# DeltaNet values transposed on VectorE through DRAM, and an instruction order laid with stored shifts of its deadlines

## The chip, the cores and the metric

The kernel runs on one core of one Trainium2 chip. The metric is the device time of one execution in microseconds (us), taken as the median over the runs shown. Differences are told against the kernel before the change, which ran on the same chip.

## The reference, cut to what matters

One layer of a decoder: 1024 tokens, width 2048, one input projection, three head groups, one output projection, and a final RMSNorm. All data are float32.

```
h = rmsnorm(x) ;  P = h @ W_in                       # columns: gMLP, DeltaNet, cross-attention
qkv = silu(causal_conv(concat(d_q, d_k, d_v)))       # depthwise, 4 taps
q, k = l2norm(q) * 128**-0.5, l2norm(k)              # 8 heads x 128
# gated delta rule over chunks, state S (128 x 128) per head:
v_new = val_c - kcd_c @ S ;  o_c = qg_c @ S + attn_c @ v_new
S = S * exp(g_last) + kd_c.T @ v_new
out_b = rmsnorm(o) * silu(d_z)
x = x + concat(out_a, out_b, out_c) @ W_out ;  y = rmsnorm(x)
```

The scan reads the values v with the tokens on the partitions, scaled per token. The convolution makes them with the channels on the partitions, so that they have to be transposed once, per head and half sequence.

## The kernel before, in words

**Matrix products.** The two large projections are seven-product (Strassen) schemes over halves of the tokens and of the columns. Each float32 factor is split into a rounded high part and a low part, and a product is three matmuls of 128x512 (high by high, high by low, low by high). The names in the trace: `raw` and `kept` are weight blocks as loaded from DRAM, `rhi` and `rlo` their split, `ll`, `lm`, `lh` the split left factors, `acc` (four) and `dn` (four) the eight PSUM banks, `obs`, `yu`, `yz` the finished sums of a projection stage. TensorE runs one product after the other; ScalarE rounds the high parts, VectorE takes the differences and adds up the seven products, and the SyncE queue (SP) issues nearly all the transfers.

**Stages.** Memory and token rows are prepared first (about 0 to 100 us). Then come the projections of the first four and the last four DeltaNet heads, a stage for the gate columns and the gMLP values (it ends near 917 us), one for the gMLP input and gate, one for the cross-attention, and the output projection. The DeltaNet work of a pair of heads and a half sequence (`hf`) is laid between the products of those stages: `front` (convolution of q and k, norms, the 128x128 matrices), `inverse` (a chain of small VectorE steps on `inv` and `sq` that solves 32x32 blocks), `levels`, `values` (the convolution of v and its transpose), `scan_step` and `heads_out`. There are eight such pairs, so sixteen calls of the convolution for v.

**Values before.** `conv` loads a head's projected columns into a buffer of the ring `xr`, forms the four taps into a buffer of the ring `tn` (one ScalarE and three VectorE instructions) and applies SiLU on ScalarE. `to_tokens` transposes the four 128x128 blocks on TensorE into a PSUM bank, and `by_token` scales them from PSUM into `vs` on ScalarE, from where the scan reads them.

**A second way to transpose, already there.** `turn` transposes the 32x32 blocks of a tile in one VectorE instruction and stores the result in DRAM with one transfer; `turned_in` reads it back with four transfers that put the blocks in their places. `heads_out` takes the scan's output through it (DRAM tensors `od`), from token rows to channel rows; `four` is the view of a tile as 4 by 4 blocks.

**What sets the order.** All instructions are recorded first (`Plan.add`) with a price. `Plan.lay` then lays them with a list scheduler: on each engine the ready instruction with the smallest key goes first. The key is the deadline that `Plan.late` works out backwards from the last order. `Plan.issue` repeats this eight times, keeps the shortest order by the planner's own costs, and emits the instructions in it, engine by engine. Each engine then works strictly in that order and waits for semaphores. Every recorded instruction carries the line of `issue` (L398) in the profile, so groups are told apart by tile names.

Of the kernel before, what the change touches and what calls it, by code (L numbers as in the profile page):

```python
# [11 lines left out]
AF = mybir.ActivationFunctionType  # L12
# [5 lines left out]
P = 128  # L18
# [4 lines left out]
HT = 512  # L23
# [3 lines left out]
NG, NH, NX = 4, 8, 4  # L27
# [26 lines left out]
class Engine:  # L54
    def __init__(self, plan, eng, ns):
        self.plan, self.eng, self.ns = plan, eng, ns
# [6 lines left out]
class Plan:  # L63
# [3 lines left out]
    DMA_RATE = 350.0  # L67
    DMA_FIXED = 3800.0
    SWITCH = 250.0
    FIRST, SPREAD, PASSES, STRETCH, AHEAD = 0, 1.75, 8, 1.25, 1000.0  # L70
    TABLE, HOLD = 1300.0, 6000.0

    def __init__(self, nc):
        self.ops = []
# [247 lines left out]
    def late(self, preds):  # L322
# [56 lines left out]
                    heapq.heappush(soon[lead.eng], (ready[lead.idx], lead.idx))  # L379
        return goal  # L380

    def issue(self):
        preds = [[] for _ in self.ops]
        for o in self.ops:
            for s in o.succ:
                preds[s.idx].append(o)
        best = None
        key, hold = [o.cls for o in self.ops], 0.3
        for n in range(self.FIRST + self.PASSES + 1):
            end = self.lay([o.cls * 1.0e9 + o.idx if o.cls < 0 else k for o, k in zip(self.ops, key)], hold)  # L390
            if best is None or end < best[0]:
                best = end, [o.at for o in self.ops]
            key, hold = self.latest() if n < self.FIRST else self.late(preds), self.HOLD
        for o, o.at in zip(self.ops, best[1]):
            pass
        self.ops.sort(key=lambda o: (o.at, o.idx))
        for o in self.ops:
            o.fn(*o.args, **o.kw)  # L398
# [3 lines left out]
def kernel(  # L402
# [21 lines left out]
    x, mem, w_in, out = x[0], mem[0], w_in[0], out[0]  # L424
# [56 lines left out]
    def tok(ap):  # L481

        return ap.rearrange("p (t c) -> p t c", c=P)
# [22 lines left out]
    jk = C([P, HT], "jk", mybir.dt.bfloat16)  # L506
# [4 lines left out]
    turn = {"acc": 0, "tp": 0, "dn": 0}  # L511
# [224 lines left out]
    for mt in range(2):  # L736
        t = [ring["ai"](F32R) for _ in range(2)]
# [9 lines left out]
    for h in range(NX):  # L747
        t = ring["vs"](F32R).rearrange("p (s m) -> p s m", s=2)
# [60 lines left out]
    def over(bufs):  # L809
        r = Ring("", 0, None)  # L810
        r.bufs = bufs
        return r
# [38 lines left out]
    r3, ww = ([steps[:, i * P : (i + 1) * P] for i in two] for two in ((0, 1), (2, 3)))  # L851
    scs = [C([P, 12, NT, NH], f"sc{hf}") for hf in range(2)]
    gcs, ecs = ([DT([NT, NH, P], f"{n}{hf}") for hf in range(2)] for n in ("gcd", "ecd"))
    e_d = [[DT([P, NT, P], f"ed{hf}_{h}") for h in range(NH)] for hf in range(2)]
    scan_banks, work = dnr.bufs[0:2], over(dnr.bufs[0:2])
    dnab = over(scan_banks)
# [90 lines left out]
    def conv(which, h, hf, o):  # L947
        ct = which * NH + h
        xr = ring["xr"]()
        w = [cw[:, k * 24 + ct : k * 24 + ct + 1] for k in range(4)]  # L950
        if hf == 0:
            G.memset(xr[:, 0:3], 0.0)
            Q.dma_start(xr[:, 3:], p_d[which][h][:, 0:HT])
        else:
            Q.dma_start(xr, p_d[which][h][:, HT - 3 :])
        S.activation(o, xr[:, 3:], AF.Copy, scale=w[3])
        for k in range(3):
            V.scalar_tensor_tensor(o, xr[:, k : k + HT], w[k], o, op0=ALU.mult, op1=ALU.add)
        S.activation(o, o, AF.Silu)

    def by_token(o, src, scale):
        for tt in range(NT):
            S.activation(o[:, tt], src[:, tt], AF.Copy, scale=scale[:, tt : tt + 1])

    def sumsq(o, src):
        for tt in range(NT):
            S.activation(jk[:, 0:P], src[:, tt], AF.Square, accum_out=o[:, tt : tt + 1])

    def qk(h, hf, tiles, hs, gt, bank):

# [188 lines left out]
    def heads_out(hf, hp, hss, rest):  # L1159
        obs = [vs for kd, ai, vs in rest]  # L1160

        for hs, ob in zip(hss, obs):
            sumsq(hs[:, 5], ob)
            V.scalar_tensor_tensor(hs[:, 6], hs[:, 5], 1.0 / P, hs[:, 0], op0=ALU.mult, op1=ALU.add)
            rsqrt_to(hs[:, 7], hs[:, 6])
            by_token(ob, ob, hs[:, 7])
        for h, (kd, ai, vs) in zip(hp, rest):
            kd, ai, y = (t.rearrange("p t c -> p (t c)") for t in (kd, ai, vs))
            turn(kd, y, o_d[hf][h])
            if h >= NJ:  # L1170
# [11 lines left out]
    def front(p, hf, banks):  # L1182

        hp = (2 * p, 2 * p + 1)
        gt = ring["gt"]().rearrange("p (h t i) -> p h t i", h=2, i=P)
        for i, h in enumerate(hp):
            tiles, hs = front_sets(), ring["hs"]()
            conv(1, h, hf, tiles[1])
            conv(0, h, hf, tiles[0])
            qk(h, hf, tiles, hs, gt[:, i], banks[i])  # L1190
            V.tensor_copy(late_hs[:, hf, h], hs[:, 0:5:4])
            for d, t in zip(late_d[hf][h], tiles[:4]):
                Q.dma_start(d, t)
# [20 lines left out]
    def values(hf, hp, gt, qs, ks, hss, rest, inv):  # L1214
        for i, h in enumerate(hp):
            v = ring["tn"]()
            conv(2, h, hf, v)
            bank = scan_banks[i]
            by_token(rest[i][2], to_tokens((v, bank))[0], hss[i][:, 4])

    def back(hf, hp, gt, qs, ks, hss, rest, inv, ut=None):
        ut = ut or levels(gt, *inv)
# [64 lines left out]
    ORDER, FIRST, SUM = (2, 1, 6, 5, 3, 7, 4), (1, 7, 2), {5: 0, 6: 1, 7: 2, 3: 3}  # L1287
# [388 lines left out]
    scan_banks, work = dnr.bufs[0:2], over(dnr.bufs[2:3])  # L1676
# [20 lines left out]
    seen = set()  # L1697
# [224 lines left out]
```

## Time and profile before

| what | value |
|---|---|
| median of 3 runs | 1594.31 us (1592.87 to 1595.48) |
| the profiled execution | 1593.81 us |
| its span, first to last instruction | 1592.1 us, mean granted TensorE clock 0.997 |
| TensorE busy | 1570.2 us, 99% |
| VectorE busy | 1228.7 us, 77% |
| ScalarE busy | 963.3 us, 61% |
| DMA | 434.12 MB, main queue 83.3% of 16 engines' time |

The engine shares are averages over the whole span. A matmul's busy time is modelled and overlaps the next one's, so the idle time of TensorE is read from the waits and from the starts of its instructions, not from the busy share alone.

### The profile page before, as it was taken

Reading aid. Unit: us, or ns where it says so; the run is one execution under the profiler, and the core shown is the slowest. Engines: PE = TensorE matmul, PEld = TensorE weight load, DVE = VectorE, ACT = ScalarE, POOL = GpSimd, SP = SyncE. Lnnn points to the kernel's source line nnn. Section 1 sums busy time; section 2 is a strip of 40 time slices with the busy share of each in tenths; the row PEclk is TensorE's granted clock in tenths of the full one; section 3 lists DMA queues with packets and bytes.
Section 4 is the critical chain, followed back from the end, with each engine's and each line's share of the span. In section 5 each row is a group of like instructions: output and inputs, shape, how many; then the busy total and the mean of one; then the engine's idle time right before and its main releaser. Section 6 shows DMA issues by size and latency. Waiting matters only on the chain.

```text
span 1592.1 us, 24568 instructions
## 1 busy us (share of the span) xinstructions
PE 1570.2 (99%) x8349; PEld 1315.3 (83%) x8349; DVE 1228.7 (77%) x1818; ACT 963.3 (61%) x2006; POOL 106.7 (7%) x143
## 2 busy tenths in 40 slices
PE   8999999999999999999999989999999999999997
PEld 7988888888887888888888878888888888888886
DVE  6977655877589997777789996867658888688875
ACT  6833255535698436787886557765658864344455
POOL 0100010001000100111111001000000000000001
PEclk9999999999999999999999999999999999999999
DMA  9999966888679898786888988999877989778647
GB/s 320 327 317 346 284 171 183 294 292 245 218 246 315 298 325 254 257 250 205 282 281 277 303 244 245 341 325 309 268 245 253 298 298 347 235 263 293 232 146 276
DMA packets 335951, 434.12 MB, mean 273 GB/s; under 512 B 70089, under 2 KB 160466, under 8 KB 335826
## 3 DMA queue, kind: packets, MB, share of 16 engines
q1 hardware_dynamic: 334098, 429.39, 83.3%
q0 software_dynamic: 1088, 2.10, 0.4%
q8 instruction: 66, 1.08, 0.3%
q10 hardware_dynamic: 640, 1.07, 0.2%
q14 instruction: 59, 0.48, 0.1%
HBM read 332.78 MB, written 99.16 MB: 271 GB/s over the span
## 4 chain that ended last, share of the span: by engine, by line
PE 92%; ACT 3%; DMA 2%; DVE 1%; issue 1%; SPq 0%; POOL 0%; POOLq 0%; ACTq 0%; DVEq 0%
PE acc L398 56%; PE dn L398 35%; ACT jk L398 1%; ACT rhi L398 1%; DMA h0d<-tn 1%; SPq L398 0%; DMA tn<-vd 0%; DMA ut<-in_x_dram 0%; DMA kept<-in_mem_dram 0%; DVE rlo L398 0%; DMA raw<-in_w_in_dram 0%; DVE vs L398 0%; ACT vs L398 0%; DVE tn L398 0%; ACT inv L398 0%
## 5 line engine op out<-in xcount | busy, mean ns | idle before, releaser
L398 PE MATMUL acc<-lh,rhi 128*128 128x512 f32 x1024 | 396.2, 396 | 2.9 <-DVE obs L398 1.2
L398 PE MATMUL acc<-lh,rlo 128*128 128x512 f32 x1024 | 382.9, 397 | 0.0
L398 ACT CAST rhi<-raw 128x1024 fp32r<-128x1024 f32 (+1 forms) x148 | 186.6, 1261 | 248.8 <-PE dn L398 133.8
L398 DVE TENSOR_TENSOR rlo<-raw,rhi 128x1024 fp32r<-128x1024 f32 (+1 forms) x148 | 219.3, 1482 | 109.0 <-ACT rhi L398 98.8
L398 PE MATMUL acc<-ll,rhi 128*128 128x512 f32 x688 | 268.0, 395 | 0.8 <-DVE ll L398 0.8
L398 PEld LDWEIGHTS acc<-lh,rhi 128*128 128x128 f32 x1024 | 192.3, 188 | 41.1 <-issue 1.5
L398 PEld LDWEIGHTS acc<-lh,rlo 128*128 128x128 f32 x1024 | 191.9, 188 | 37.4
L398 DVE TENSOR_TENSOR ll<-ll,lh 128x1024 fp32r<-128x1024 f32 x122 | 148.5, 1217 | 17.3 <-ACT lh L398 17.0
L398 PEld LDWEIGHTS acc<-ll,rhi 128*128 128x128 f32 x688 | 129.6, 189 | 26.4 <-DVE ll L398 1.3
L398 ACT CAST lh<-ll 128x1024 fp32r<-128x1024 f32 x122 | 128.2, 1051 | 29.5 <-PE dn L398 9.0
L398 PE MATMUL acc<-lm,rhi 128*128 128x512 f32 x336 | 130.6, 394 | 0.0
L398 PE MATMUL dn<-lh,rhi 128*128 128x512 f32 x288 | 112.6, 393 | 0.0
L398 PE MATMUL dn<-lh,rlo 128*128 128x512 f32 x288 | 109.7, 393 | 0.0
L398 DVE TENSOR_TENSOR raw<-raw,kept 128x1024 f32<-128x1024 f32 (+1 forms) x56 | 80.9, 1444 | 6.9 <-DMA raw<-in_w_in_dram 5.9
L398 DVE TENSOR_TENSOR rlo<-kept,rhi 128x1024 fp32r<-128x1024 f32 (+1 forms) x29 | 41.8, 1443 | 47.3 <-ACT rhi L398 44.4
L398 PE MATMUL dn<-ll,rhi 128*128 128x512 f32 x192 | 75.2, 393 | 0.0
L398 PEld LDWEIGHTS acc<-lm,rhi 128*128 128x128 f32 x336 | 63.2, 188 | 11.9
L398 ACT CAST rhi<-kept 128x1024 fp32r<-128x1024 f32 (+1 forms) x29 | 35.6, 1229 | 50.3 <-PE dn L398 26.2
L398 PEld LDWEIGHTS dn<-lh,rhi 128*128 128x128 f32 x288 | 54.1, 188 | 10.6
L398 PEld LDWEIGHTS dn<-lh,rlo 128*128 128x128 f32 x288 | 54.0, 188 | 10.5
L398 POOL TENSOR_TENSOR hs<-hs,mhalf 128x4 f32<-128x4 f32 x32 | 48.4, 1515 | 195.3 <-DVE hs L398 194.9
L398 POOL TENSOR_TENSOR small<-small,mhalf 128x1 f32<-128x1 f32 x26 | 21.6, 832 | 562.8 <-DVE small L398 562.8
(421 smaller groups left out, 3449.6 us busy)
## 6 DMA issues: line engine op xcount, KB each, us to landing
raw<-in_w_in_dram SPq DMA_DIRECT2D x120, 512.0 KB
ll<-hsd SPq DMA_DIRECT2D x54, 512.0 KB
raw<-in_w_out_dram SPq DMA_DIRECT2D x48, 512.0 KB
raw<-in_w_in_dram SPq DMA_DIRECT2D x72, 256.0 KB
lm<-hsd SPq DMA_DIRECT2D x26, 512.0 KB
pd<-obs SPq DMA_DIRECT2D x48, 256.0 KB
late<-os SPq DMA_DIRECT2D x44, 256.0 KB
kept<-in_w_in_dram SPq DMA_DIRECT2D x20, 512.0 KB
```

What stands on the lines that cost most here:

```text
L398: o.fn(*o.args, **o.kw)
```

## The change

**Values.** `values` no longer uses TensorE. After the convolution, VectorE transposes the 32x32 blocks of v into the `xr` buffer that the convolution has finished reading, that buffer is stored to a new DRAM tensor (`vt_d`, `vtd` in the trace), four transfers read it back into the same `tn` buffer with the tokens on the partitions, and `by_token` scales it from SBUF, through the blocked view, into `vs`.

```
         for k in range(3):
             V.scalar_tensor_tensor(o, xr[:, k : k + HT], w[k], o, op0=ALU.mult, op1=ALU.add)
         S.activation(o, o, AF.Silu)
+        return xr[:, 0:HT]
...
     def by_token(o, src, scale):
         for tt in range(NT):
-            S.activation(o[:, tt], src[:, tt], AF.Copy, scale=scale[:, tt : tt + 1])
+            S.activation(like(o[:, tt], src), src[:, tt], AF.Copy, scale=scale[:, tt : tt + 1])
...
             v = ring["tn"]()
-            conv(2, h, hf, v)
-            bank = scan_banks[i]
-            by_token(rest[i][2], to_tokens((v, bank))[0], hss[i][:, 4])
+            t = conv(2, h, hf, v)
+            turn(t, v, vt_d[hf][h])
+            turned_in(v, vt_d[hf][h])
+            by_token(rest[i][2], four(v, "b t i"), hss[i][:, 4])
```

**Order.** The planner makes sixteen passes in place of eight. The best order's deadlines are then shifted by a stored table of 169 numbers, each the seed of one shift, and the order is laid once more with the shifted keys. A shift adds noise to the deadlines in a stretch of the order, or pulls one instruction with its forerunners ahead, or pushes one with its followers back.

```
-    FIRST, SPREAD, PASSES, STRETCH, AHEAD = 0, 1.75, 8, 1.25, 1000.0
+    FIRST, SPREAD, PASSES, STRETCH, AHEAD = 0, 1.75, 16, 1.25, 1000.0
     TABLE, HOLD = 1300.0, 6000.0
+    WIDTHS = (4.0e3, 8.0e3, 16.0e3, 24.0e3, 40.0e3, 60.0e3, 90.0e3, 140.0e3)
+    NUDGES = (
+        13843793, 3460882, 26541279, 31820011, 28477318, 13031908, 5917944, 33473397, 35532666,
...
+    def nudged(self, preds, end, at, key):
+
+        key = list(key)
+        heads = sorted((at[o.idx], o.idx) for o in self.ops if o.lead is o and o.cls >= 0)
+        for n in self.NUDGES:
+            kind, s = n >> 24, n & 0xFFFFFF
...
+            if kind:
+                t0, i = heads[int(draw() / 2.0**24 * len(heads))]
...
+                    key[o.idx] += -reach if kind == 1 else reach
...
+                if draw() / 2.0**24 < share:
+                    key[i] += reach * (draw() + draw() + draw() - 1.5 * 2.0**24) / 2.0**23
+        return key
...
-        for o, o.at in zip(self.ops, best[1]):
-            pass
+        self.lay(self.fixed(self.nudged(preds, *best)), self.HOLD)
```

The new order differs nearly everywhere by some places. Three places follow, as the program has them before and after.

**TensorE at the first pair's values and scan.** `tn` is v, `ut` the inverse, `vs` the scaled values. Before:

```order
L398 MATMUL dn_114<-lh,rhi_76 128x512
L398 MATMUL dn_114<-ll,rhi_76 128x512
L398 MATMUL dn_111<-ident,tn_86 128x128 x4
L398 MATMUL dn_114<-lh,rlo_74 128x512
L398 MATMUL acc_107<-lh,rhi_77 128x512
```

After:

```order
L464 MATMUL dn_111<-ut_82,y_338 128x64 x4
L464 MATMUL acc_110<-lh,rhi_76 128x512
L464 MATMUL dn_113<-lh,rhi_76 128x512
L464 MATMUL dn_113<-ll,rhi_76 128x512
L464 MATMUL dn_113<-lh,rlo_74 128x512
L464 MATMUL acc_109<-lh,rlo_74 128x512
L464 MATMUL acc_110<-ll,rhi_76 128x512
L464 MATMUL dn_111<-vs_412,ut_82 128x128
```

The group of four transposes is gone, and the scan's first product with `vs` follows the products of `levels` with nothing of v ahead of it on TensorE.

**VectorE at the end of the gate stage (near 917 us).** `obs<-acc` takes a finished sum out of a bank that the next product needs; `raw_72<-dn` are four steps of the gMLP weights behind which TensorE's products `dn<-raw,ones` wait; `inv` and `sq` are the inverse. Before:

```order
L398 TENSOR_TENSOR obs<-acc_110,yu 128x512
L398 BN_STATS small_105<-sm 128x6
L398 TENSOR_TENSOR sq<-inv_488,inv_489 128x192
L398 BN_AGGR small_106<-small_105 128x2
L398 TENSOR_TENSOR rlo_75<-raw_73,rhi_77 128x1024
L398 TENSOR_SCALAR small_106<-small_106 128x1
L398 TENSOR_TENSOR inv_489<-inv_489,sq 128x8x24
L398 TENSOR_TENSOR raw_72<-dn_112,utri 128x128
L398 TENSOR_TENSOR sq<-inv_488,inv_489 128x175
L398 TENSOR_SCALAR sm<-sm,small_106 128x512
L398 TENSOR_TENSOR inv_489<-inv_489,sq 128x7x25
L398 TENSOR_TENSOR raw_72<-dn_112,utri 128x128
```

After:

```order
L464 TENSOR_TENSOR rlo_75<-raw_73,rhi_77 128x1024
L464 TENSOR_TENSOR inv_505<-inv_505,sq 128x2x30
L464 TENSOR_TENSOR ll<-ll,lh 128x1024
L464 TENSOR_TENSOR sq<-inv_504,inv_505 128x31
L464 TENSOR_TENSOR raw_72<-dn_112,utri 128x128
L464 TENSOR_TENSOR inv_505<-inv_505,sq 128x31
L464 TENSOR_TENSOR raw_72<-dn_112,utri 128x128
L464 COPY inv_504<-inv_505 128x32x32
L464 TENSOR_TENSOR raw_72<-dn_112,utri 128x128
L464 TENSOR_TENSOR raw_72<-raw_72,kept_80 128x1024
L464 TENSOR_TENSOR raw_72<-dn_112,utri 128x128
```

The inverse has moved ahead by six of its 31 steps, so that it ends here, and the difference `ll` of the next left factor has moved in front of the four gMLP steps. (The buffer numbers changed with the new tensors.)

**TensorE at the same place.** `acc` are the sums of the stage that begins, `ones` a tile of ones. Before:

```order
L398 MATMUL acc_109<-lh,rhi_77 128x512
L398 MATMUL acc_110<-lh,rhi_77 128x512
L398 MATMUL dn_112<-raw_72,ones 128x128
L398 MATMUL acc_107<-ll,rhi_77 128x512
L398 MATMUL acc_107<-lh,rlo_75 128x512
```

After:

```order
L464 MATMUL acc_110<-lh,rlo_75 128x512
L464 MATMUL acc_110<-lh,rhi_77 128x512
L464 MATMUL dn_112<-raw_72,ones 128x128
L464 MATMUL acc_110<-ll,rhi_77 128x512
L464 MATMUL acc_107<-lh,rlo_75 128x512
```

The first `dn<-raw,ones` now stands near the end of this step of the product, behind the `ll` products of the first three banks; before it stood ahead of all of them.

**SP at the values of the fourth pair (second half sequence, heads 2 and 3).** `xr<-pd` loads the columns of v, `od<-kd` is the scan's output on its way through DRAM. Before:

```order
L398 DMA xr_91<-pd_3_174 128x515
L398 DMA late_7_3_218<-os 128x512
L398 DMA raw_73<-in_w_in_dram 128x2x512
L398 DMA ll<-hsd_320 128x2x512
L398 DMA raw_73<-in_w_in_dram 128x2x256
L398 DMA od_0_267<-kd_394 128x512
```

After:

```order
L464 DMA lm<-hsd_320 128x2x512
L464 DMA vtd_2_355<-xr_90 128x512
L464 DMA vtd_3_356<-xr_91 128x512
L464 DMA od_0_267<-kd_410 128x512
L464 DMA od_1_268<-kd_415 128x512
L464 DMA tn_86<-vtd_2_355 32x4x128 x3
L464 DMA tn_87<-vtd_3_356 32x4x128 x2
L464 DMA tn_86<-vtd_2_355 32x4x128
L464 DMA tn_87<-vtd_3_356 32x4x128 x2
L464 DMA kd_415<-late_3_2_233 128x512
L464 DMA kd_410<-late_2_2_229 128x512
```

Two stores and eight loads of the values have come in, the loads three and more places behind their store, and the next loads of the matmuls' factors stand behind them.

More of the change, by code (lines that the diff above doesn't have):

```diff
@@ L1 @@
+import bisect
 import heapq
@@ L69 @@
     SWITCH = 250.0
-    FIRST, SPREAD, PASSES, STRETCH, AHEAD = 0, 1.75, 8, 1.25, 1000.0
+    FIRST, SPREAD, PASSES, STRETCH, AHEAD = 0, 1.75, 16, 1.25, 1000.0
     TABLE, HOLD = 1300.0, 6000.0
+    WIDTHS = (4.0e3, 8.0e3, 16.0e3, 24.0e3, 40.0e3, 60.0e3, 90.0e3, 140.0e3)
+    NUDGES = (
[19 rows of a table added]
+    )
     def __init__(self, nc):
@@ L380, in late, with fixed, draw @@
         return goal
+    def fixed(self, key):
+        return [o.cls * 1.0e9 + o.idx if o.cls < 0 else k for o, k in zip(self.ops, key)]
+    def nudged(self, preds, end, at, key):
[3 more added lines that the diff above has]
+            kind, s = n >> 24, n & 0xFFFFFF
+            def draw():
+                nonlocal s
+                s = (s * 1664525 + 1013904223) & 0xFFFFFFFF
+                return s >> 8
+            draw(), draw()
+            if kind:
+                t0, i = heads[int(draw() / 2.0**24 * len(heads))]
+                width = 0.5 * self.WIDTHS[draw() >> 21]
+                reach = 2.0 ** (8 + (draw() >> 21))
+                seen, todo = {i}, [i]
+                while todo:
+                    o = self.ops[todo.pop()]
+                    key[o.idx] += -reach if kind == 1 else reach
+                    for x in (o, *o.tail):
+                        for q in preds[x.idx] if kind == 1 else x.succ:
+                            q = q.lead
+                            near = at[q.idx] > t0 - width if kind == 1 else at[q.idx] < t0 + width
+                            if q.idx not in seen and q.cls >= 0 and near:
+                                seen.add(q.idx)
+                                todo.append(q.idx)
+                continue
+            first = draw() / 2.0**24 * end
+            last = first + self.WIDTHS[draw() >> 21]
+            reach = 2.0 ** (8 + (draw() >> 21))
+            share = ((draw() >> 21) + 1) / 16
+            for t, i in heads[bisect.bisect_left(heads, (first, -1)) :]:
+                if t >= last:
+                    break
+                if draw() / 2.0**24 < share:
+                    key[i] += reach * (draw() + draw() + draw() - 1.5 * 2.0**24) / 2.0**23
+        return key
     def issue(self):
@@ L389, in issue @@
         for n in range(self.FIRST + self.PASSES + 1):
-            end = self.lay([o.cls * 1.0e9 + o.idx if o.cls < 0 else k for o, k in zip(self.ops, key)], hold)
+            end = self.lay(self.fixed(key), hold)
             if best is None or end < best[0]:
-                best = end, [o.at for o in self.ops]
+                best = end, [o.at for o in self.ops], key
             key, hold = self.latest() if n < self.FIRST else self.late(preds), self.HOLD
-        for o, o.at in zip(self.ops, best[1]):
-            pass
+        self.lay(self.fixed(self.nudged(preds, *best)), self.HOLD)
         self.ops.sort(key=lambda o: (o.at, o.idx))
@@ L853 @@
     gcs, ecs = ([DT([NT, NH, P], f"{n}{hf}") for hf in range(2)] for n in ("gcd", "ecd"))
+    vt_d = [[DT([P, HT], f"vtd{hf}_{h}") for h in range(NH)] for hf in range(2)]
     e_d = [[DT([P, NT, P], f"ed{hf}_{h}") for h in range(NH)] for hf in range(2)]
@@ L959, in conv, with like @@
         S.activation(o, o, AF.Silu)
+        return xr[:, 0:HT]
     def by_token(o, src, scale):
         for tt in range(NT):
-            S.activation(o[:, tt], src[:, tt], AF.Copy, scale=scale[:, tt : tt + 1])
+            S.activation(like(o[:, tt], src), src[:, tt], AF.Copy, scale=scale[:, tt : tt + 1])
     def sumsq(o, src):
         for tt in range(NT):
-            S.activation(jk[:, 0:P], src[:, tt], AF.Square, accum_out=o[:, tt : tt + 1])
+            S.activation(like(jk[:, 0:P], src), src[:, tt], AF.Square, accum_out=o[:, tt : tt + 1])
+    def like(o, src):
+        return o.rearrange("p (b i) -> p b i", b=4) if len(src.shape) == 4 else o
     def qk(h, hf, tiles, hs, gt, bank):
```

18 rows, old and new, of the table NUDGES are left out of this document.

## The prediction

> **What bounds the kernel now.** I read the busy shares first, then the windows by stage, then who TensorE waited for, then the order of time at the places where it waits.
>
> ```profile
> PE 1570.2 (99%) x8349; PEld 1315.3 (83%) x8349; DVE 1228.7 (77%) x1818; ACT 963.3 (61%) x2006; POOL 106.7 (7%) x143
> ```
>
> TensorE carries the time. The windows (length, then busy time of PE, PEld, DVE, ACT and POOL, granted clock, DMA share, GB/s) show where it is idle:
>
> ```profile
> 0.00:100.00 100.00, 93.85 (x619) 85.04 (x620) 80.01 (x143) 70.69 (x146) 9.96 (x21) 1.00 0.98 317
> 450.00:510.00 60.00, 58.35 (x300) 47.72 (x299) 55.05 (x104) 56.15 (x168) 5.63 (x7) 1.00 0.94 300
> 800.00:900.00 100.00, 100.00 (x486) 84.00 (x485) 93.26 (x157) 68.23 (x161) 11.97 (x13) 1.00 0.88 286
> 912.00:935.00 23.00, 18.90 (x75) 14.41 (x75) 22.16 (x49) 10.16 (x13) 1.24 (x2) 0.93 0.96 287
> 935.00:1000.00 65.00, 64.21 (x411) 53.31 (x409) 48.43 (x79) 45.56 (x94) 8.49 (x12) 1.00 0.83 248
> 1000.00:1100.00 100.00, 99.94 (x659) 84.33 (x660) 75.85 (x100) 66.12 (x134) 4.17 (x8) 1.00 0.98 328
> 1200.00:1592.00 392.00, 383.12 (x1761) 317.74 (x1759) 313.33 (x430) 220.19 (x378) 8.60 (x10) 0.99 0.79 266
> ```
>
> Of 1592.1 - 1570.2 = 21.9 us idle, 6.2 lie in the start, 8.9 at the end (after the last product), 4.1 in the 23 us around the end of the gate stage, 1.7 and 0.8 in two other rows, and next to nothing elsewhere. So a microsecond of TensorE's work removed after the start is a microsecond of time, unless a wait takes its place, and waits can give back about 4.1 + 1.7 + 0.8 = 6.6 us and no more outside the start and the end.
>
> **Part 1: sixteen groups of transposes leave TensorE.** The first of them in order of time:
>
> ```profile
> 616.91 0.39 PE L398 MATMUL dn<-ll,rhi 128*128 128x512 f32 x1
> 617.14 0.60 PE L398 MATMUL dn<-ident,tn 128*128 128x128 f32 x4
> 617.50 0.47 PE L398 MATMUL dn<-lh,rlo 128*128 128x512 f32 x1
> 617.81 0.39 PE L398 MATMUL acc<-lh,rhi 128*128 128x512 f32 x1
> 618.04 0.39 PE L398 MATMUL acc<-ll,rhi 128*128 128x512 f32 x1
> ```
>
> Starts count, not durations: one product takes 618.04 - 617.81 = 0.23. From the group's start to the second product after it are 617.81 - 617.14 = 0.67, in which one product is done, so the group costs 0.67 - 0.23 = 0.44. Sixteen calls give **-7.0 us**. It is all on the path, since the windows of these stages show TensorE full.
>
> **Part 2: what comes in instead.** VectorE gets sixteen block transposes, ScalarE reads v from SBUF and no longer from PSUM. The nearest rows:
>
> ```profile
> L398 DVE STREAM_TRANSPOSE kd<-vs 128x512 f32<-128x512 f32 x16 | 11.3, 704 | 4.5 <-ACT vs L398 4.5
> L398 ACT ACTIVATE vs<-vs,hs 128x128 f32<-128x128 f32 x64 | 21.0, 395 | 0.7 <-POOL hs L398 0.7
> L398 ACT ACTIVATE vs<-dn,hs 128x128 f32<-128x128 f32 x64 | 18.6, 376 | 5.3 <-PE dn L398 5.1
> ```
>
> 16 x 0.704 = 11.3 us on VectorE over some 600 us, and 64 x (0.395 - 0.376) = 1.2 us on ScalarE. Both are hidden behind TensorE at 77% and 61%; the cover is thin only where VectorE is at 93% (800 to 900) and 22.16 of 23 us (912 to 935). In the transfers there are 16 stores of 256 KB and 64 loads of 64 KB more, 8.4 MB; at 273 GB/s, the mean by the row below, that is 31 us of transfer spread over 600, 5% more where the windows stand at 0.83 to 0.98.
>
> ```profile
> DMA packets 335951, 434.12 MB, mean 273 GB/s; under 512 B 70089, under 2 KB 160466, under 8 KB 335826
> ```
>
> I take 0 for these three as work, since TensorE stays full in the very row at 0.98; what they do is to make transfers land later, which is priced next.
>
> What is new on the path of the values is the way through DRAM. The scan's output takes the same way, so one round of it is in the trace:
>
> ```profile
> 1131.09 0.71 DVE L398 STREAM_TRANSPOSE kd<-vs 128x512 f32<-128x512 f32 x1 [1.41 <-ACT vs L398]
> 1131.83 0.32 SPq L398 DMA_DIRECT2D od<-kd  x1
> 1137.48 1.87 SPq L398 DMA_DIRECT2D ai<-od  x4
> 1144.48 0.73 ACT L398 ACTIVATE kd<-ai,col 128x512 f32<-128x512 f32 x1
> ```
>
> From the transpose to the reader are 1144.48 - 1131.09 = 13.4 us, against the 0.44 of the group. The values depend on projections that are long done, so the convolution can be laid earlier; it moves ahead of the scan in the order, and the scan no longer has v's transposes just ahead of it. What stands to wait, if the loads land late, is first `by_token` on ScalarE with the roundings `rhi` and `lh` behind it, then the scan's product on TensorE and everything behind that. On SP the loads wait for their store, and the prefetch of the next factors waits with them; at the fourth pair only the other stores and one load lie between. How long TensorE stands when a transfer is late the trace shows once:
>
> ```profile
> PE acc L398 <- DVE obs L398: 1.2, 1, 1.2
> PE dn L398 <- DMA tn<-vd: 0.8, 1, 0.8
> ```
>
> One such wait in eight pairs is what I take, **+0.8 us**. From below the bound is 0 (a transfer cannot end earlier than not being waited for). From above it is a full miss, 13.4 us in each of eight pairs, 107 us, which the early convolution excludes; 1.2 us, the longest wait on this list past the start, in every pair gives 9.6, and that is the end I keep.
>
> By the Trainium skill, "VectorE: DVE Perf Modes", section "Rules for kernel authors", a 128x128 transpose belongs on TensorE if the result may land in PSUM, and VectorE's own covers 32x32 blocks. That rule speaks against this part: by it the change trades a short operation for a long way, and the third rival below is what it would come to. The trace agrees on the way (0.44 against 13.4 us) but TensorE is the engine that has no room.
>
> **Part 3: the order at the end of the gate stage.** In order of time before:
>
> ```profile
> 919.10 0.47 PE L398 MATMUL acc<-lh,rhi 128*128 128x512 f32 x1 [1.25 <-DVE obs L398]
> ...
> 928.30 0.49 PE L398 MATMUL dn<-raw,ones 128*128 128x128 f32 x2 [1.65 <-DVE raw L398]
> 929.64 0.77 PE L398 MATMUL acc<-ll,rhi 128*128 128x512 f32 x1 [0.85 <-DVE ll L398]
> 930.21 0.63 PE L398 MATMUL acc<-lh,rlo 128*128 128x512 f32 x1
> 930.63 0.63 PE L398 MATMUL acc<-lh,rhi 128*128 128x512 f32 x1
> ...
> 932.77 0.56 PE L398 MATMUL acc<-lh,rlo 128*128 128x512 f32 x1
> 933.16 0.39 PE L398 MATMUL acc<-lh,rhi 128*128 128x512 f32 x1
> ```
>
> VectorE is the late one: `dn<-raw,ones` needs the bank that four steps `raw<-dn` read, and these and `ll` stand behind `rlo`, the inverse and the norm. The idle time is 4.1. From 929.64 to 933.16 stand seven products and two small matmuls (three of the products and the small ones are in the rows left out); at 0.23 and 0.11 that is 1.8 of the 3.5 us, so a slower clock (0.93 in the window) costs some 1.5 more. The place costs 5.6 us.
>
> In the order after, I add up VectorE from the last `obs<-acc` to the fourth `raw<-dn`, by rows of before: three steps of 128x1024 (`rlo`, `ll`, `raw`) at 1.22, the `COPY` of the inverse at 1.14, one 128x512 scaling at 0.55, six steps of the inverse and the like at 0.3, four `raw<-dn` at 0.28, less 0.08 of overlap for each of fourteen: 7.1 us. The rows these come from:
>
> ```profile
> L398 DVE TENSOR_TENSOR rlo<-raw,rhi 128x1024 fp32r<-128x1024 f32 x76 | 92.7, 1219 | 49.6 <-ACT rhi L398 43.5 <-PE acc L398 4.5 <-PE dn L398 1.4
> L398 DVE COPY inv<-inv 128x1024 f32<-128x1024 f32 x2 | 2.3, 1138 | 0.0
> 926.39 0.55 DVE L398 TENSOR_SCALAR sm<-sm,small 128x512 f32<-128x512 f32 x1
> 927.53 0.28 DVE L398 TENSOR_TENSOR raw<-dn,utri 128x128 f32<-128x128 f32 x1
> ```
>
> TensorE has 27 products from the one that this `obs` frees to the first `ones`, 27 x 0.23 = 6.2. So it still waits about 1 us there, part of it already at `ll`, and it can wait once more for the sums `obs` of the other banks, which stand between larger steps: 1.25 as before. With half a microsecond of slow clock I take 2.8 us left of 5.6, **-2.8 us**. The ends are 0 left (-5.6) and as much again (+5.6).
>
> By the Trainium skill, "TensorE: Matmul & The Clock Gate", section "What's actually happening", the array falls to half its clock after an idle window of about 3.4 us. The trace agrees on the size (930.21 to 930.63, so 0.42 from start to start against 0.23) and not on the window: no wait here is longer than 1.65. By that rule alone shorter waits would change nothing in the 1.5 us; I let the slow stretch follow the waits.
>
> **Part 4: the order elsewhere.** The new order moves products, sums and transfers by some places everywhere. In the rows outside the start, the end and the stage end it can win 1.7 + 0.8 = 2.5 us at most and can lose as much as one more bad stage end, 5.6. Neither end is nearer by any row; I take 0. The start (6.2 us idle, with the transfers at 0.98) waits mostly for the first loads, whose order is fixed, and I take 0 there, with 2 us either way.
>
> **The sum.** -7.0 + 0.8 - 2.8 + 0 = -9.0 us on an execution of 1593.81 (span 1592.1, 1.7 around it), which gives 1584.8. The median of the runs, 1594.31, stands 0.5 above that execution, so 1585.3; I say 1585.
>
> **The rivals.**
>
> 1. The idle places close as well: the stage end gives all of its 5.6, the others 2.5, the start 2, no new wait. -7.0 - 5.6 - 2.5 - 2 = -17.1, 1577. For it speaks that all of these are waits of a microsecond for VectorE or ScalarE that a few places in the order mend; against it that a new order has new places like these. Chance 0.22.
>
> 2. VectorE takes it back: it is nearly full at 800 to 935 already and gets some of the sixteen transposes there, so the stage end stays at 5.6 and there are two new waits of 0.8. -7.0 + 1.6 = -5.4, 1589. Chance 0.15.
>
> 3. Slower: the loads of the values miss the scan, as the rule of the skill would have it. The deciding price is 9.8 / 8 = 1.2 us of standing per pair, with part 1 and part 3 given. If each of the pairs stands 2 us, the sum is -9.8 + 16 = +6.2, 1600. For it speaks the fourth pair, where the loads stand right behind their stores on SP; against it that the order leaves the round of 13.4 us elsewhere. Chance 0.08.
>
> 4. It does not do what it says: the transposes go, but the new order opens as many waits as the 7 us. 1594, within 0.2%. Chance 0.07.
>
> The forecast itself (1580 to 1588) has 0.48.
>
> **How the numbers follow.** 0.2% of 1594 is 3.2 us, about what a measurement of this kernel can tell from no change: faster means below 1591.1. The forecast, rival 1 and most of rival 2 lie there, 0.48 + 0.22 + 0.14 = 0.84; rival 4 with the edge of rival 2, 0.08; rival 3, 0.08. The range leaves out rival 3 and the far side of rival 1: it goes from 1575, just below -17.1, to 1592, where +5.6 of part 4 and a little more of part 2 have used up most of part 1.
>
> **What would show it.** Part 1: TensorE has 64 transposes fewer and its busy time falls by about 7 us while its idle time does not grow. Part 2: the group of `xr<-tn` transposes on VectorE at 0.7 us each; in who waited for whom, TensorE behind ScalarE's `vs` or behind a transfer `tn<-vtd` by 1 us or less. Part 3: in the 23 us around the end of the gate stage less than 3 us idle, and a clock near 1. The prediction is wrong if TensorE's list of waits shows `vs`, `rhi` or `ll` with several us, or if the start's idle time changes by more than 2 us.

## The result, and the profile after

The changed kernel takes 1583.78 us (median of 4 runs, 1582.32 to 1584.43) against 1593.78 us of the kernel before on the same chip: a ratio of 0.993, 95% interval 0.992 to 0.9945. The profiled execution took 1582.32 us, its span is 1580.3 us; before it was 1592.1. So the two traces differ by 11.8 us, the medians by 10.0.

The busy times of the whole span, after (before: TensorE 1570.2 x8349, VectorE 1228.7, ScalarE 963.3; 434.12 MB):

```profile
PE 1561.2 (99%) x8285; PEld 1308.2 (83%) x8285; DVE 1240.5 (79%) x1834; ACT 962.7 (61%) x2004; POOL 99.9 (6%) x143
...
DMA packets 347470, 442.49 MB, mean 280 GB/s; under 512 B 71369, under 2 KB 169938, under 8 KB 347346
```

TensorE has the 64 transposes fewer and 9.0 us less busy time; its idle time went from 21.9 to 19.1. VectorE has 11.8 us more, the transfers 8.4 MB more. The windows after, in the columns of the prediction (length; PE, PEld, DVE, ACT, POOL; granted clock, DMA share, GB/s):

```profile
0.00:100.00 100.00, 95.04 (x630) 86.50 (x631) 79.47 (x142) 72.47 (x148) 8.68 (x21) 1.00 1.00 322
450.00:510.00 60.00, 59.52 (x303) 49.74 (x302) 58.42 (x101) 54.56 (x161) 3.63 (x5) 1.00 0.95 307
800.00:900.00 100.00, 100.00 (x462) 83.14 (x461) 94.19 (x159) 60.28 (x112) 8.06 (x10) 1.00 0.93 292
912.00:935.00 23.00, 22.35 (x159) 17.44 (x159) 20.16 (x37) 13.83 (x19) 2.15 (x4) 1.00 0.82 244
935.00:1000.00 65.00, 60.80 (x375) 50.53 (x365) 46.84 (x75) 37.80 (x83) 6.47 (x9) 0.97 0.82 249
1200.00:1580.00 380.00, 371.96 (x1709) 308.31 (x1707) 304.06 (x415) 209.75 (x358) 4.99 (x8) 0.99 0.79 265
```

At the end of the gate stage (912 to 935) the idle time fell from 4.1 to 0.65 us and the clock is whole. In the next row it rose, from 0.8 to 4.2 us, with the clock at 0.97. Who TensorE waited for there, and the one long wait for a load of the values, on ScalarE:

```profile
PE dn L464 <- DVE sq L464: 2.1, 1, 2.1
PE dn L464 <- DVE states L464: 1.8, 1, 1.8
...
ACT rhi L464 <- DMA tn<-vtd: 4.4, 1, 4.4
```

**The place where time went back.** In the order of time after, first the queue of SP, then the engines:

```profile
955.30 2.62 SPq L464 DMA_DIRECT2D sm<-gvd  x4
957.97 2.05 SPq L464 DMA_DIRECT2D tn<-vtd  x4
...
966.10 0.91 SPq L464 DMA_DIRECT2D tn<-vtd  x2
967.11 0.40 SPq L464 DMA_DIRECT2D raw<-in_w_in_dram  x1
...
968.59 4.15 SPq L464 DMA_DIRECT2D sm<-gvd  x4
...
972.95 1.23 DVE L464 TENSOR_TENSOR kept<-raw,kept 128x1024 f32<-128x1024 f32 x1 [3.88 <-DMA raw<-in_w_in_dram]
...
975.23 0.75 DVE L464 SCALAR_TENSOR_TENSOR sq<-dn,col,raw 128x512 f32<-128x512 f32 x1
...
976.02 1.03 PE L464 MATMUL dn<-raw,tn 128*128 128x128 f32 x6 [2.06 <-DVE sq L464]
977.15 0.79 PE L464 MATMUL acc<-lm,rhi 128*128 128x512 f32 x1
977.75 0.63 PE L464 MATMUL acc<-lh,rlo 128*128 128x512 f32 x1
978.17 0.63 PE L464 MATMUL acc<-lh,rhi 128*128 128x512 f32 x1
978.60 0.63 PE L464 MATMUL dn<-raw,tn 128*128 128x128 f32 x2
...
980.24 0.39 PE L464 MATMUL acc<-ll,rhi 128*128 128x512 f32 x1
980.46 0.39 PE L464 MATMUL acc<-lh,rhi 128*128 128x512 f32 x1
```

The transfer engines in the five microseconds ahead of that issue (columns as above):

```profile
960.00:965.00 5.00, 5.00 (x32) 4.42 (x31) 2.62 (x4) 3.81 (x9) 0.20 (x1) 1.00 0.38 98
```

The weight block `raw` is issued at 967.11, behind an almost unbroken row of small issues on SP, six of them loads of the values in the last nine microseconds. The transfer engines are busy 0.38 in the five microseconds before, so that up to its issue the block is held back by the queue and not by the bytes; what fills the time from issue to landing is not shown. VectorE takes it 5.8 us later, having stood 3.88 us; `sq` stands behind that on VectorE, and TensorE waits 2.06 us for `sq`. The products after it start 0.42 apart and not 0.23: from 977.15 to 980.24 stand six products and two small matmuls (part of them in the rows left out), which is 1.6 us at 0.23 and 0.11, so the slow clock costs 1.5 more.

The other late block, for which VectorE stood 2.21 us up to 945.79 and TensorE then 1.80 us for `states`, is issued at 938.88; between 930.71 and that issue SP has fifteen other transfers, none of them of the values. So only the second late block stands behind the values' loads.

**A ladder of starts.** Since TensorE runs an almost unchanged number of instructions, the timeline gives a second account: the start of the n-th TensorE instruction (transposes of the values not counted). The stretches from the start of the span to number 300, from there to 750, to 2850 and to the last of them, in us, each from the one profiled execution of a kernel (the experiments follow below):

| kernel | to 300 | 300 to 750 | 750 to 2850 | 2850 to last |
|---|---|---|---|---|
| before | 52.6 | 75.4 | 458.7 | 996.0 |
| after | 52.2 | 73.4 | 456.9 | 989.1 |
| after, no shifts (16 passes) | 52.8 | 75.4 | 458.6 | 990.1 |
| after, no shifts, 8 passes | 51.4 | 76.1 | 458.6 | 989.6 |
| after, three weight blocks ahead | 52.4 | 73.4 | 456.9 | 985.5 |
| after, values read back in one load | 54.2 | 73.4 | 456.9 | 983.0 |
| after, block transposes twice | 52.2 | 73.4 | 456.9 | 985.9 |
| before, one transpose of four kept | 54.3 | 75.4 | 459.1 | 991.5 |
| before, transposes left out | 54.1 | 75.4 | 458.7 | 997.0 |
| old values in the new order | 53.4 | 73.4 | 456.9 | 1004.0 |
| new values in the old order | 54.3 | 75.8 | 462.8 | 1041.7 |

The last stretch begins near 587 us, before the first scan, and holds all the transposes. From before to after it gave 6.9 us, the two middle ones 2.0 and 1.8, the first 0.4; behind the last product lie 0.7 more. The first stretch differs by up to 2 us between kernels whose order is the same there, so that its 0.4 cannot be told from chance.

### The profile page after: what moved, and what is told of

It is laid out like the page before. It is cut to its first block, busy times and chain, and to the rows that moved or that the text cites. A ratio compares the mean times of both kernels' runs of the same rounds, so it can differ in the third digit from the quotient of the medians.

```text
span 1580.3 us, 24539 instructions
## 1 busy us (share of the span) xinstructions
PE 1561.2 (99%) x8285; PEld 1308.2 (83%) x8285; DVE 1240.5 (79%) x1834; ACT 962.7 (61%) x2004; POOL 99.9 (6%) x143
## 2 busy tenths in 40 slices
DMA packets 347470, 442.49 MB, mean 280 GB/s; under 512 B 71369, under 2 KB 169938, under 8 KB 347346
## 4 chain that ended last, share of the span: by engine, by line
PE 95%; DMA 2%; SPq 1%; DVE 1%; ACT 1%; issue 1%; POOL 0%; POOLq 0%; ACTq 0%; DVEq 0%
PE acc L464 58%; PE dn L464 37%; SPq L464 1%; DMA raw<-in_w_in_dram 0%; DMA kept<-in_mem_dram 0%; DMA vd<-sm 0%; DMA late<-os 0%; DMA sm<-gvd 0%; DVE kept L464 0%; DVE os L464 0%; ACT vs L464 0%; ACT rhi L464 0%; DVE rlo L464 0%; ACT jk L464 0%; ACT L464 0%
## 5 line engine op out<-in xcount | busy, mean ns | idle before, releaser
L464 PE MATMUL acc<-lh,rhi 128*128 128x512 f32 x1024 | 387.0, 396 | 0.6 <-ACT rhi L464 0.6
L464 PE MATMUL acc<-ll,rhi 128*128 128x512 f32 x688 | 263.0, 395 | 0.0
L464 DVE TENSOR_TENSOR lm<-lm,lh 128x1024 fp32r<-128x1024 f32 x42 | 51.3, 1221 | 11.6 <-ACT lh L464 11.5
```

## Experiments

All ran in five rounds beside the kernel before; a ratio is to that. In the kernels that take another kernel's order, the planner's result is replaced by a stored order (the other kernel's places as keys of a sort by dependences). The edits are shortened to what they do.

**Old values in the new order.** The kernel before, with each group of transposes put just ahead of `by_token`:

```
-        (planner of before)
+        key[o] = place of o in the order after     # transposes: just ahead of their by_token
```

> The values go through TensorE as before the change, and everything else stands in the order of after, the groups of four transposes just ahead of the scaling of the values. Theory A (the sixteen groups are 7.0 us of a full TensorE, and the order is worth the rest): the median is that of after plus 7, 1591, so 2 to 4 us below before. Rival B (the gain is the order's alone, since the transposes filled gaps that TensorE had anyway): within 1.5 us of after, 1584 to 1585. Rival C (the order is worth nothing without the values' new way): 1593 to 1594, as before.

Measured: 1597.99 us, ratio 1.0027 (1.0017 to 1.0036), above every value expected. The ladder shows what is what: the first three stretches are those of the new order, and the last one is 8 us longer than before. TensorE's waits:

```profile
PE dn L606 <- ACT vs L606: 4.5, 6, 1.2
PE dn L606 <- ACT steps L606: 3.4, 3, 2.5
```

Placed just ahead of their reader, the transposes leave TensorE waiting for ScalarE's scaling: the last stretch is 14.9 us longer than in the changed kernel, of which the transposes themselves are 7.0 by part 1's price. In that order v is ready long before (15 us or more, see below), so an earlier place was open; it was not tried. The run shows that this placing loses, not that the order fits the new way alone.

**New values in the old order.** The block transposes at the end of SiLU, store and loads right behind:

```
-        (planner and shifts of after)
+        key[o] = place of o in the order before    # transpose: end of SiLU, store +1 us, loads +4 us
```

> The values go through VectorE and DRAM as after the change, and everything else stands in the order of before; the block transposes stand where SiLU ends, the stores 1 us and the loads 4 us behind them. In the trace of before 6 us lie between the first group of transposes and the scan's first product with the values, and a round through DRAM took 13.4. Theory A (the way through DRAM is only free because the order after the change starts the convolution early): up to 7.4 us of standing in each of eight pairs, less 7.0 saved: 1600 to 1645, slower than before. Rival (the scan has slack in any order): 1586 to 1589.

Measured: 1644.09 us, ratio 1.031 (1.030 to 1.033).

```profile
PE dn L668 <- DVE steps L668: 14.4, 2, 8.8
PE acc L668 <- ACT rhi L668: 7.5, 3, 5.1
PE dn L668 <- ACT vs L668: 6.1, 1, 6.1
...
745.03 1.28 ACT L668 ACTIVATE vs<-tn,hs 128x128 f32<-128x128 f32 x4 [6.48 <-DMA tn<-vtd]
...
811.76 1.28 ACT L668 ACTIVATE vs<-tn,hs 128x128 f32<-128x128 f32 x4 [11.11 <-DMA tn<-vtd]
...
1017.99 1.28 ACT L668 ACT_TABLE_LOAD   x1 [7.54 <-DMA vd<-sm]
```

The long way through DRAM, at the place of the short one, costs 50 us. The waits for `steps` are the scan behind late values, since ScalarE's scaling stands 6 to 11 us for the loads `tn<-vtd`, and the 5.1 us for `rhi` stand behind the same scaling: the mechanism of the third rival. The 6.1 us for `vs` are another thing: a copy `vs<-dn` of the scan, behind a step on ScalarE that stood 7.54 us for the transfers `vd<-sm`, which share SP's queue with the values' loads there. So not all of the 50 us are late values, but the change depends on an order that starts the values early. In the changed kernel, by the view of the tile `tn` (count, shortest, median and longest duration, first and last start):

```profile
L464 DVE STREAM_TRANSPOSE xr<-tn x16: 672/705/712, 509.3 to 1130.8; 128x512 f32<-128x512 f32 x16
...
L464 ACT ACTIVATE vs<-tn,hs x64: 384/390/425, 553.5 to 1152.1; 128x128 f32<-128x128 f32 x64
```

The first values are read 44 us after their transpose, the last ones 21 us, and the shortest of the sixteen ways takes 15 us (transpose at 746.2, first reader at 761.1).

**No shifts.** The changed kernel with the sixteen passes, without the stored shifts, and then with eight passes:

```
-    NUDGES = ( 169 numbers )
+    NUDGES = ()
...
-        self.lay(self.fixed(self.nudged(preds, *best)), self.HOLD)
+        for o, o.at in zip(self.ops, best[1]):
+            pass
```

> The values as after the change, the order from the planner's sixteen passes without the stored shifts. Theory A (the transposes are 7.0 of the gain of about 10, the shifts are worth the rest by having fewer waits): 1587 (1585 to 1590), TensorE's idle time outside start and end 3 to 8 us. Rival (the shifts carry most of it, since an unshifted order misses late transfers): 1591 or more. Rival (the shifts are worth nothing on the chip): 1584, as after.

> The kernel after with neither the stored shifts nor the eight more passes of the planner: the best order of 8 passes is kept. The sixteen passes without shifts gave 1589.2. Theory A, the passes beyond the eighth bring little: 1588 to 1591, so all of the new values' way and none of the order's choice. Theory B, the new way needs the longer search: 1594 or more, with TensorE waiting for `vs` or for transfers `tn<-vtd` by several us.

Measured: 1589.16 us, ratio 0.9969 (0.9959 to 0.9979), and with eight passes 1589.00, ratio 0.9964 (0.9951 to 0.9976). Both are as their theory A had it. The eight passes more bring nothing. The new way of the values with the planner's own order brings 5 us, the shifts 5.4 more. By the ladder 3.8 of these lie between the 300th and the 2850th instruction, where nothing of the values' transposes is on TensorE, and 1.0 in the last stretch.

**Three weight blocks ahead.** The order after; three loads of `raw` moved ahead on SP (in the trace two of them stand right in front of a group of four `sm<-gvd`, at 930.03 and 939.24, the third in front of a `ut<-udrb` and three `tn<-vtd`, at 964.80):

```
+        for i, ahead_of in ((8955, 7440), (8986, 7454), (9017, 7744)):
+            rank[i] = rank[ahead_of] - 0.5
```

> The order of after with three weight blocks moved ahead on the SyncE queue, near 930 to 970 us: two ahead of a group of four small loads each, one by eight places. In the trace of after VectorE stood 2.2 and 3.9 us for two of these blocks, and TensorE 1.8 and 2.1 us behind it, with 1.5 us or so of slower clock. Theory A (the blocks are late because the SyncE queue is full of small issues there): both waits of TensorE go, 3 to 5 us, 1579 to 1581. Rival (the blocks are late because the transfers are full, or something else is next in line): within 1.5 us of after, 1583 to 1585.

Measured: 1580.48 us, ratio 0.9919 (0.9906 to 0.9933). As theory A had it, TensorE no longer waits for `states` or `sq`; the window and VectorE's step:

```profile
935.00:1000.00 65.00, 62.35 (x445) 51.52 (x445) 46.57 (x74) 40.33 (x87) 6.46 (x9) 1.00 0.82 249
...
969.61 1.23 DVE L676 TENSOR_TENSOR kept<-raw,kept 128x1024 f32<-128x1024 f32 x1 [1.39 <-DMA raw<-in_w_in_dram]
```

VectorE stands 1.39 us and not 3.88. It is the fastest kernel that computes everything, 3.3 us under the changed one, though the two intervals overlap a little.

**Values read back in one load.** 64 loads of 64 KB become 16 of 256 KB, in the same order:

```
-        for b in range(4):
-            Q.dma_start(o[b * 32 : (b + 1) * 32].rearrange("j (a n) -> j a n", a=4), v[b])
+        Q.dma_start(o, src)             # values only, at the place of the first of the four
```

> The kernel after, in its own order, with the values of a head read back in one transfer of 256 KB in place of four of 64 KB: 48 issues fewer on SP, the same bytes (the placing of the blocks is left out of the computation). Theory A, it is the number of issues on SP that makes the weight blocks `raw<-in_w_in` at 940 to 980 us late, on which VectorE's `kept` and then TensorE's products wait: those waits (1.8 and 2.1 us) shrink under 1 us, 1580 to 1582. Theory B, the transfers' bytes or the store's own way make them late: no change, 1583 to 1585.

Measured: 1577.95 us, ratio 0.9894 (0.9881 to 0.9907), 5.8 us under the changed kernel and below what theory A gave; the wait for `sq` is gone, the one for `states` is 1.1 us. The bytes are the same, so it is not the bytes. But the run changes two things: there are 48 issues fewer, and the pieces are four times as long (340559 packets in place of 347470). The queue and VectorE at the same place:

```profile
955.52 2.62 SPq L466 DMA_DIRECT2D sm<-gvd  x4
958.19 0.62 SPq L466 DMA_DIRECT2D tn<-vtd  x1
...
965.03 0.40 SPq L466 DMA_DIRECT2D raw<-in_w_in_dram  x1
...
970.87 1.23 DVE L466 TENSOR_TENSOR kept<-raw,kept 128x1024 f32<-128x1024 f32 x1 [2.09 <-DMA raw<-in_w_in_dram]
```

The block is issued 2.1 us earlier, with two loads of the values ahead of it since 955 us in place of six, and taken 2.1 us earlier, 5.8 us after its issue as before. So here the gain is in the queue; for the other places issues and packets are not told apart. Followed finer, the ladder gains 5.4 us against the changed kernel between 903 and 985 us, and 0.6 at 1100. The trace of the next run, with every issue left in place, gains 3.2 us too, so the size is to be taken from the medians.

**Block transposes twice.** VectorE's new work doubled, in the order after:

```
-            o.fn(*o.args, **o.kw)
+            for _ in range(1 + (o is a block transpose of the values)):
+                o.fn(*o.args, **o.kw)
```

> The kernel after, in its own order, with each of the sixteen block transposes of the values issued twice on VectorE (the second writes the same again). It doubles VectorE's new work, 11.2 us more. Theory A, that work is hidden behind TensorE: 1584 to 1586, no new wait of TensorE over 1 us. Theory B, VectorE's time is on the path: about 1595. Theory C, only what falls where VectorE is nearly full (800 to 1000 us, some six of the sixteen) adds: 1587 to 1589, with waits for VectorE's steps there.

Measured: 1582.91 us, ratio 0.9928 (0.9915 to 0.9941), the same as the changed kernel.

```profile
L466 DVE STREAM_TRANSPOSE xr<-tn 128x512 f32<-128x512 f32 x32 | 22.5, 705 | 0.9 <-ACT tn L466 0.3
```

Theory A: 11.4 us more on VectorE cost nothing that the interval of some 4 us can show. Its runs lie between 1579.41 and 1586.24, and in the profiled one (the shortest) TensorE waited 0.9 us for `sq` and not 2.1: how late the block at 967 us is differs from one execution to the next.

**Transposes left out of the kernel before.**

```
-            by_token(rest[i][2], to_tokens((v, bank))[0], hss[i][:, 4])
+            by_token(rest[i][2], v.rearrange("p (t i) -> p t i", i=P), hss[i][:, 4])
```

> The kernel before, in its own order, with the sixty-four TensorE transposes of the values taken out and nothing in their place: `by_token` reads v from SBUF as the convolution left it (the turning of the values is left out of the computation). Theory A, TensorE's work counts one for one: sixteen groups of 0.44 us less, 7.0 us, about 1587, TensorE's busy time down by 7 and its idle time as before (21.9 us). Theory B, in the old order the freed time is lost again in waits for ScalarE or VectorE: 1591 to 1594, with idle time on TensorE up by 3 to 7 us. Theory C, the transposes cost more than the 0.44 because the scan's next product also waited for what reads their bank: 1580 to 1584.

Measured: 1594.64 us, ratio 1.0006 (0.9997 to 1.0014): nothing gained, as theory B had it. The place is one:

```profile
1030.60 0.72 ACT L599 ACTIVATE tn<-xr,cw 128x512 f32<-128x512 f32 x1
...
1037.02 0.76 PE L599 MATMUL acc<-lh,rhi 128*128 128x512 f32 x1 [4.23 <-DVE obs L599]
1037.58 0.63 PE L599 MATMUL acc<-ll,rhi 128*128 128x512 f32 x1
1038.00 0.63 PE L599 MATMUL acc<-lh,rhi 128*128 128x512 f32 x1
```

In the kernel before, ScalarE formed the first tap of the next convolution at 1022:

```profile
1022.23 1.34 ACT L398 ACTIVATE tn<-xr,cw 128x512 f32<-128x512 f32 x2 [1.74 <-PE dn L398]
```

My edit moved it to 1030.60, because `by_token` now reads the buffer `tn` itself and so holds it longer. VectorE's later taps stand ahead of `obs` in its order, TensorE waited 4.23 us and ran eight products at about 0.42: followed finer, the ladder loses 6.8 us here and had gained 4.2 before it. So this run did not price the transposes alone, and the next one repairs it.

**One transpose of four kept.** The buffer is read by TensorE as before:

```
-            by_token(rest[i][2], to_tokens((v, bank))[0], hss[i][:, 4])
+            PE.transpose(bank[:, 0:P], v[:, 0:P], ident)
+            by_token(rest[i][2], tok(bank), hss[i][:, 4])
```

> The kernel before, in its own order, with one of the four TensorE transposes of each group of values kept and three taken out; `by_token` reads the same PSUM bank as before (three quarters of the values are left out of the computation). Other than with all of them taken out, the convolution's buffer `tn` comes free at TensorE's read, as in the kernel before. A group falls from 0.44 to 0.11 us: 16 x 0.33 = 5.3 us less work on TensorE. Theory A, the microseconds are worth their full size while nothing else is moved, and what ate them with all four taken out was `tn` held until `by_token`: 1588 to 1590, and no wait for `obs` near 1030 us beyond those of before (1.2 us). Theory B, the old order gives freed time back in waits anyway: 1592 to 1595, with a wait of some us near 1030 us again.

Measured: 1590.76 us against 1595.94 of the kernel before on that chip, ratio 0.9967 (0.9954 to 0.998): 5.2 us (3.2 to 7.3), of 5.3 expected by theory A. The wait for `obs` is 0.9 us:

```profile
PE acc L599 <- DVE obs L599: 0.9, 1, 0.9
```

## Why the prediction was right, point by point

The time (1585 said, 1583.8 measured) came out by terms of which two were mis-sized in opposite directions. That it came within 1.2 us is in part luck.

**Part 1 (-7.0).** Right. One transpose of four kept gave 5.2 of 5.3 us, with an interval of 3.2 to 7.3. The last stretch of the ladder, with all of the transposes in it, gave 6.9; parts 2 and 3 lie in it too and cancel, as follows.

**Part 2, VectorE and ScalarE (0).** Right. The groups after:

```profile
L464 DVE STREAM_TRANSPOSE xr<-tn 128x512 f32<-128x512 f32 x16 | 11.1, 700 | 0.7 <-ACT tn L464 0.7
...
L464 ACT ACTIVATE vs<-tn,hs 128x128 f32<-128x128 f32 x64 | 21.6, 392 | 0.8 <-DMA tn<-vtd 0.5 <-DMA mixd<-vs 0.3
```

700 ns against 704 taken, 392 against 395, and doubling VectorE's part changed nothing, which rules the second rival out. The rule that a 128x128 transpose belongs on TensorE if the result may land in PSUM ("VectorE: DVE Perf Modes", "Rules for kernel authors", in the Trainium skill) does not hold here in an order laid for the new way: 0.70 us on an engine with room and a hidden round through DRAM beat 0.44 us on the one without. In the old order it lost by 50 us.

**Part 2, the transfers (+0.8).** The step that failed. I priced bytes (31 us of transfer, hidden) and a wait of the scan for the values. TensorE never waited for `vs` or `tn<-vtd`. What cost time was the values' place in SP's queue: 80 issues more, among them 64 loads, and behind some of them weight blocks. With 48 of them gone 5.8 us go, with the same bytes and the same order; with three weight blocks moved ahead and all issues kept, 3.3. I had named SP's queue for the next factors at the fourth pair, and gave it no price. The 80 issues are not late blocks in themselves: between 903 and 985 us SP issues 119 transfers before the change and 120 after it, so what stands ahead of a block counts.

**Part 3 (-2.8).** The place gave more, 5.6 to 0.65 us, so -4.9. But 20 to 60 us later the late blocks took it back: 3.4 us more idle time in the next window, and 1.5 of slow clock. About 2.06 + 1.5 of that stand behind the values' loads, the 1.80 us for `states` behind other transfers. Parts 2 and 3 together are 0.0 where I had -2.0.

**Part 4 (0).** Mis-sized the other way: -0.4 in the first stretch, -2.0 and -1.8 in the middle ones, all before the first scan, and the two middle ones by the shifts alone. In the start I had said that it waits for the first loads, whose order is fixed. Up to the 300th instruction no run speaks against that; after it, in the kernel before, TensorE waited for roundings and sums, which an order can mend:

```profile
67.52 0.66 PE L398 MATMUL dn<-ident,kept 128*128 128x128 f32 x4 [0.23 <-ACT kept L398]
...
72.99 0.39 PE L398 MATMUL dn<-ahi,rhi 128*128 128x256 f32 x1 [0.65 <-DVE tn L398]
```

Neither is left after; they are 0.9 of the 2.0 us, and where the rest lies is not shown. The sum by measured terms is -7.0 + 0.0 - 0.4 - 2.0 - 1.8 - 0.7 (behind the last product) = -11.9, against 11.8 between the traces; the 0.4 in it is no larger than what two executions differ by.

**The rivals.** The first (idle places close too) came true in the start and between 450 and 510 us (1.65 us idle before, 0.5 after), but not its condition that no new wait comes. The third is real, with 1644 us in the old order, and the laying averts it. The fourth did not come.

What stays open: why the same weight block is late by different amounts in different executions, what fills the 5.8 us from its issue to its reader, whether issues or packets count in the load in one piece, and how far SP's order could be mended further. Of the three blocks moved, none was moved alone.

## What to carry to other kernels

Where one engine is full, price a removed instruction by the starts around it and take it at full size, but only after asking which buffer it released and when. Price added transfers by their time on the issuing queue, not by bytes alone, and look for what is queued behind them: a late weight block cost more here than the values' own way. A longer way was free here only with an order that starts it early, so a change of way and a change of order are one change, and each has to be tried with the other's absence.

## What the runs showed that I had not expected

**How well a stretch repeats.** The 300th to the 750th instruction of TensorE took 73.40 to 73.42 us in all five kernels of the new order, on two chips at least; the stretch up to the 300th varied among the same five from 52.2 to 54.2. So a single trace tells differences of 0.1 us in that stretch, and 2 us of noise sit in the first 50.

**The clock after a wait.** A wait of 2.06 us (976.02 above) was followed by half clock, one of 4.23 us (1037.02) too, and one of 1.80 us (950.13), in the changed kernel too, was not. The granted clock changes in these traces only at steps of 3.41 us, so the windows here begin and end at such steps, first in the changed kernel, then in the kernel before:

```profile
946.01:949.42 3.41, 2.32 (x13) 1.63 (x11) 3.41 (x4) 1.08 (x5) 0.00 (x0) 1.00 0.77 199
949.42:952.84 3.42, 2.71 (x16) 2.40 (x17) 3.13 (x7) 1.25 (x1) 0.00 (x0) 1.00 1.04 327
973.32:976.73 3.41, 1.35 (x12) 1.16 (x11) 3.41 (x4) 1.17 (x7) 0.00 (x0) 1.00 0.52 127
976.73:980.14 3.41, 3.31 (x11) 2.54 (x10) 3.04 (x10) 2.91 (x11) 1.02 (x1) 0.50 1.05 315
...
926.29:929.70 3.41, 0.91 (x5) 0.36 (x3) 3.41 (x11) 1.04 (x1) 0.07 (x1) 1.00 1.07 252
929.70:933.12 3.42, 3.42 (x9) 2.82 (x10) 3.25 (x8) 1.05 (x1) 0.00 (x0) 0.50 0.91 309
```

The wait of 2.06 us lies whole in one window, and the next window has half clock. The wait of 1.80 us is cut by a border into 1.09 and 0.71, and the clock stays. In the kernel before, the waits of 1.65 and 0.85 us fall into one window, with 2.5 us idle. Counted so over all eleven traces, between the start and the last product, the clock fell after every window in which TensorE was idle 1.9 us or more (eleven times), and after none with 1.6 or less. So what two short waits cost in these traces depends on whether they fall into the same window.

"TensorE: Matmul & The Clock Gate", section "What's actually happening" (the Trainium skill), gives an idle window of about 3.4 us for the fall and as long a busy one for the return. The traces agree on the length and on the return, after one window in the changed kernel; for the fall a window that was idle for part of its length was enough.

**What an issue on SP takes.** Single small loads hold the queue some 0.4 us (`tn<-vtd`: median 0.43), and groups of four took 2.05 to 4.15 us in the rows above; why some groups take twice as long as others is not shown. Here the queue was almost unbroken while the transfer engines were at 0.38 (960 to 965).
